# The down projection's left sums of a Winograd-Strassen scheme, formed in the gate and up stage instead of the down stage

## The chip, the cores and the metric

The kernel runs on one core of a Trainium2 chip. What counts is the device time of one execution, in microseconds (us): the median of the runs shown.

## What is computed

Two encoder layers on 1024 tokens of width 1024. Each has a token mixer (a Fourier part, a gated part, attention) and a channel mixer, of which this text speaks:

```python
def swiglu(h, w_gate, w_up, w_down):
    return (jax.nn.silu(h @ w_gate) * (h @ w_up)) @ w_down

x = x + rmsnorm(swiglu(rmsnorm(x, g_pre_ffn[l]), w_gate[l], w_up[l], w_down[l]), g_post_ffn[l])
```

The hidden width is 2816, that is 22 blocks of 128 or 11 pairs of blocks. All is float32.

## The kernel before

**Products.** A float32 operand is split into a high half (a rounding cast on ACT, L119) and a low half (operand minus high half, on DVE, L120). A product is three matmuls, high by high, high by low, low by high (`matmul3`, L142 to L144). `split` at L118 is used everywhere, so its two lines stand for all stages, and a tile's name tells which: `w_f` is a weight of gate or up, `dw` an operand of the down projection.

**Seven products for eight.** The three matrices of the channel mixer are multiplied by a Winograd form of Strassen's scheme: operands are cut into 2 x 2 blocks, sums and differences of blocks are formed, and seven products, numbered v = 1 to 7 in the down stage, replace eight.

**The gate and up stage.** `NPROD` = 154 products: 11 pairs `p`, each with j = 0 to 13 (v = j // 2, gate and up by turns). `ff_load` fetches the weights of a pair in four tiles from a pool of four buffers (`rawp`), `ff_sums` (L943) forms the sums of weight blocks on POOL, `ff_prep` splits a weight six products ahead into a pool of nine buffers (`Wp`), `ff_prod` multiplies into PSUM (`fx`, `fy`), `ff_post` empties the accumulators into slots of `nat` (L997, L1006), applies silu, multiplies gate by up and stores the four blocks of the pair's result in the DRAM tile `asp` (`store_a`, L974).

**The down stage.** The 11 pairs make four groups (3, 3, 3, 2 pairs). In each group the seven products go in the order v = 1, 2, 5, 6, 3, 7, 4: 28 steps (`STEPS`). A step is for each of four row blocks `u` one accumulator, with three matmuls for each pair of the group: 36 matmuls, 24 in the last group (`d_prod`). `X` accumulators (`fX`) are opened at v = 1, `Y` accumulators (`fY`) at v = 2 and anew at v = 5; there are four banks of each kind. They are emptied into `nat` on ACT (L1121) or added to it on DVE (L1123). `d_load` (L1051) fetches for each pair two tiles of 128 x 1024 of the left side, from `asp`, and two of `w_down`, into a ring of buffers of which four are those of `rawp`. `d_sums` (L1064) forms the sums on POOL, in place:

```python
                if v == 5:
                    tt(a(11), a(11), a(21))
                    tt(a(21), a(21), a(22), ALU.add)
                    tt(w(11), w(12), w(11))
                    tt(w(12), w(22), w(12))
                elif v == 6:
                    tt(a(21), a(22), a(11))
                    tt(w(11), w(22), w(11))
                elif v == 3:
                    tt(a(12), a(12), a(21))
                elif v == 4:
                    tt(w(21), w(21), w(11))
```

That is eight sums a pair, four of left blocks `a` and four of right blocks `w`. `d_prep(s + 3)` runs behind step s: it forms the sums of step s + 3 and splits its operands, two for each pair, into 18 buffers, so an operand's buffer is one that step s has just left.

**What sets the order.** The program's order as written, and a scheduler that orders each engine's instructions when the kernel is built; `run_behind` and `chain` pin some. Each engine, and SP's queue of DMA issues, then works through its list in order. In the last group, the final normalisation (`Residual`, L177 to L228) is woven into the steps by the table `FIN`.

Of the kernel before, what the change touches and what calls it, by code (L numbers as in the profile page):

```python
# [81 lines left out]
def encoder_kernel(ctx, tc, A, out):  # L82
# [273 lines left out]
    for l in range(DEPTH):  # L356
# [613 lines left out]
            pcn[0] += 1  # L970
            return nat[:, i, half * 512:(half + 1) * 512]

        def store_a(i, half, t):
            nc.sync.dma_start(asp[i * P:(i + 1) * P, half * 512:(half + 1) * 512], t)  # L974

        def ff_prod(n):
            p, j = divmod(n, 14)
# [11 lines left out]
        def ff_post(n):  # L989
            p, j = divmod(n, 14)  # L990
            v, m = j // 2, j % 2
            X = pq["X", p, m]

            def finish(key, acc, i, half):

                t = pq[key, p, m]
                nc.vector.tensor_tensor(out=t, in0=acc, in1=t, op=ALU.add)  # L997
                if m == 0:
                    nc.scalar.activation(t, t, AF.Silu)
                else:  # L1000
                    nc.vector.tensor_tensor(out=t, in0=pq[key, p, 0], in1=t, op=ALU.mult)
                    store_a(i, half, t)

            if v in (0, 3, 4):
                t = pq[("p1", None, None, "u2", "u3")[v], p, m] = pc()
                nc.scalar.copy(t, X)  # L1006
            if v == 1:
                finish("p1", pq["Y", p, m], 2 * p, 0)
            elif v == 4:
                finish("u3", pq["Z", p, m], 2 * p + 1, 1)  # L1010
            elif v == 5:
                if m == 0:
                    t = pq["s", p] = pc()
                    nc.scalar.activation(t, X, AF.Silu)
                else:
                    t = pq["s", p]
                    nc.vector.tensor_tensor(out=t, in0=X, in1=t, op=ALU.mult)
                    store_a(2 * p + 1, 0, t)
            elif v == 6:
                finish("u2", pq["Z", p, m], 2 * p, 1)  # L1020

        DGROUPS = ((0, 1, 2), (3, 4, 5), (6, 7, 8), (9, 10))
        DORD = (1, 2, 5, 6, 3, 7, 4)
        STEPS = [(gi, v) for gi in range(len(DGROUPS)) for v in DORD]
        draw, dop, dps, du = {}, {}, {}, {}
# [5 lines left out]
        RING = [("dR", i) for i in range(9)] + [("raw", 0)] * 4 + [("dM", i) for i in range(10)]  # L1033

        def d_raw_slot(gi, n):

            return RING[(12 * gi + n) % len(RING)]

        def d_load(gi, n):

            G = len(DGROUPS[gi])
            j, r = divmod(n, 2 * G)
            pi, side = divmod(r, 2)
            i = 2 * DGROUPS[gi][pi] + j
            kind, slot = d_raw_slot(gi, n)
            nm = f"dr{l}_{gi}_{n}"
            if kind == "raw":
                raw = rawp.tile([P, S], F32, tag="raw", name=nm)
            else:
                raw = d_unit(kind, slot, [S], F32, nm)  # L1050
            nc.sync.dma_start(raw, (A["w_down"][l] if side else asp)[i * P:(i + 1) * P, :])  # L1051
            draw[gi, pi, side, j] = raw

        def d_blk(gi, pi, side, b):

            r, c = divmod(b, 10)
            j, h = (c, r) if side == 0 else (r, c)
            return draw[gi, pi, side, j - 1][:, (h - 1) * 512:h * 512]

        def d_sums(gi, v):  # L1060
            for pi in range(len(DGROUPS[gi])):
                a = lambda b: d_blk(gi, pi, 0, b)
                w = lambda b: d_blk(gi, pi, 1, b)
                tt = lambda o, x, y, op=ALU.subtract: nc.gpsimd.tensor_tensor(out=o, in0=x, in1=y, op=op)  # L1064
# [12 lines left out]

        DOPER = {1: (11, 11), 2: (12, 21), 5: (21, 11), 6: (21, 11), 3: (12, 22), 7: (11, 12), 4: (22, 21)}

        def d_op_slot(s, n):  # L1080

            gi, v = STEPS[s]
            if len(DGROUPS[gi]) == 3:
                return ("W", "W", "W", "W", "W", "W", "W", "W", "W", ("dO", 0), ("dO", 1), ("dO", 2),
                        ("dO", 3), ("dN", 0), ("dN", 1), ("dN", 2), ("dN", 3), ("dN", 4))[s % 3 * 6 + n]
            return {1: "W", 2: "W", 5: ("dO", n), 6: ("dN", n), 3: ("dR", 4 + n), 7: ("dR", n), 4: ("dN", n)}[v]

        def d_prep(s):
            if s >= len(STEPS):
                return  # L1090
            gi, v = STEPS[s]
            d_sums(gi, v)
            n = 0
            for pi in range(len(DGROUPS[gi])):
                for side in range(2):
                    slot = d_op_slot(s, n)
                    nm = f"dw{l}_{s}_{n}"
                    if slot == "W":
# [82 lines left out]
        for n in range(NPROD):  # L1181
            p, j = divmod(n, 14)
            ff_prod(n)
            if n > 4:
                ff_post(n)
            if n in (0, 2):
                b_tp(6 + n // 2)
            for e in TSTEPS.get(n, ()):
                run_behind(e)
            if j in LOADS and p + 1 < NPAIR:  # L1190
                ff_load(p + 1, *LOADS[j])
            if n > 7:
                ff_prep(n + 6)
            if n == NPROD - 10:
                sB.close()
                sL = ExitStack()
                du["dR"] = pool(f"dR{l}", 1, "left", sL)
            if NPROD - 10 <= n < NPROD - 1:
                d_load(0, n - (NPROD - 10))
            if n == NPROD - 1:  # L1200
                for k in range(9, 12):
                    d_load(0, k)
        sT.close()


        last = l == DEPTH - 1
        sD = ExitStack()
        du["dO"] = pool(f"dO{l}", 1, "left", sL)
        du["dN"] = pool(f"dN{l}", 1, "right", sD)
        du["dM"] = pool(f"dM{l}", 1, "right", sD)  # L1210
        for s in range(3):
            d_prep(s)

        fin = {}

# [36 lines left out]
        for s, (gi, v) in enumerate(STEPS):  # L1252
            end = gi + 1 == len(DGROUPS)
            for u in range(4):
                if not (end and v == 4):
                    d_tile(s, u)
                if end and v == 7:
                    d_tile(s + 1, u)
            k = DORD.index(v)
            if not end and k < 4:  # L1260
                for n in range(k * 3, min(k * 3 + 3, 4 * len(DGROUPS[gi + 1]))):
# [49 lines left out]
```

## Time and profile before

| | |
|---|---|
| median of 3 runs | 2284.11 us (2282.67 to 2284.31) |
| the profiled execution | 2282.25 us, span 2280.5 us |
| PE busy | 2191.5 us, 96% of the span |
| DVE busy | 1607.3 us, 70% |
| ACT busy | 1138.5 us, 50% |
| POOL busy | 952.2 us, 42% |
| DMA queue of SP | 178.70 MB, 23.1% of 16 engines' span |

Engines: PE is TensorE's matmuls, DVE is VectorE, ACT is ScalarE, POOL is GpSimd, SP is SyncE, which issues the DMAs. Matmuls are pipelined, so one of 0.39 us starts every 0.23 us and a busy PE is not PE at its peak: how many matmuls start in a stretch tells more. The first layer's gate and up stage runs from about 460 to 894 us, its down stage to about 1115; the second layer's down stage begins at about 2028. The rows are at the end of this part.

### The profile page before, as it was taken

Reading aid. Unit: us, or ns where it says so; the run is one execution under the profiler, and the core shown is the slowest. Engines: PE = TensorE matmul, PEld = TensorE weight load, DVE = VectorE, ACT = ScalarE, POOL = GpSimd, SP = SyncE. Lnnn points to the kernel's source line nnn. Section 1 sums busy time; section 2 is a strip of 40 time slices with the busy share of each in tenths; the row PEclk is TensorE's granted clock in tenths of the full one; section 3 lists DMA queues with packets and bytes.
Section 4 is the critical chain, followed back from the end, with each engine's and each line's share of the span. In section 5 each row is a group of like instructions: output and inputs, shape, how many; then the busy total and the mean of one; then the engine's idle time right before and its main releaser. Section 6 shows DMA issues by size and latency. Waiting matters only on the chain. (4 is left out here: it accounts for less than half of the span.)

```text
span 2280.5 us, 29159 instructions
## 1 busy us (share of the span) xinstructions
PE 2191.5 (96%) x10460; PEld 1807.2 (79%) x10460; DVE 1607.3 (70%) x2457; ACT 1138.5 (50%) x2188; POOL 952.2 (42%) x797
## 2 busy tenths in 40 slices
PE   9999999999999999999899999999999999999986
PEld 7787888878888888877677788888788888877874
DVE  6868986585444447899977698965854444488998
ACT  6338996553333334434452489855533333344333
POOL 2643443243323235655637235332432323266556
PEclk9999999999999999999999999999999999999998
DMA  4110003213132316221331000042132323253212
GB/s 159 42 45 20 19 10 115 99 65 106 61 105 62 104 62 240 111 84 47 107 111 38 17 19 20 10 138 85 61 102 74 93 74 93 74 226 111 83 47 111
DMA packets 104961, 185.28 MB, mean 81 GB/s; under 512 B 12272, under 2 KB 62704, under 8 KB 104816
## 3 DMA queue, kind: packets, MB, share of 16 engines
q1 hardware_dynamic: 103376, 178.70, 23.1%
q0 software_dynamic: 1440, 4.72, 0.7%
q8 instruction: 82, 1.34, 0.2%
q14 instruction: 63, 0.52, 0.1%
HBM read 143.54 MB, written 39.85 MB: 80 GB/s over the span
## 5 line engine op out<-in xcount | busy, mean ns | idle before, releaser
L144 PE MATMUL fx<-hT,w_f 128*128 128x512 f32 x1584 | 374.9, 393 | 6.6 <-ACT nat L1006 4.5
L144 PEld LDWEIGHTS fx<-hT,w_f 128*128 128x128 f32 x1584 | 300.1, 190 | 71.2 <-ACT nat L1006 6.0
L120 DVE TENSOR_TENSOR w_f<-raw_f,w_f 128x512 fp32r<-128x512 f32 x264 | 213.9, 814 | 192.6 <-ACT w_f L119 189.5
L120 DVE TENSOR_TENSOR dw<-dr,dw 128x512 fp32r<-128x512 f32 x300 | 325.4, 1129 | 30.2 <-ACT dw L119 29.9
L144 PE MATMUL z<-w_z,hT 128*128 128x512 f32 x1152 | 286.3, 403 | 11.8 <-DVE rz L196 5.1
L119 ACT CAST dw<-dr 128x512 fp32r<-128x512 f32 x308 | 171.8, 618 | 234.5 <-POOL dr L1064 94.1
L119 ACT CAST w_f<-raw_f 128x512 fp32r<-128x512 f32 x264 | 162.2, 621 | 236.3 <-PE fy L144 196.7
L144 PEld LDWEIGHTS z<-w_z,hT 128*128 128x128 f32 x1152 | 216.6, 193 | 58.6 <-DVE rz L196 5.5
L144 PE MATMUL fX<-dw,dw 128*128 128x512 f32 x1056 | 248.5, 391 | 8.8 <-DVE nat L1123 8.5
L943 POOL TENSOR_TENSOR s<-raw_f,raw_f 128x512 f32<-128x512 f32 x44 | 58.9, 1338 | 459.5 <-DMA raw_f<-in_w_gate_dram 442.1
L144 PE MATMUL fy<-hB,w_f 128*128 128x512 f32 x1056 | 248.0, 390 | 1.9 <-DVE hB L120 1.9
L144 PEld LDWEIGHTS fX<-dw,dw 128*128 128x128 f32 x1056 | 197.1, 188 | 54.8 <-DVE nat L1123 13.9
L144 PEld LDWEIGHTS fy<-hB,w_f 128*128 128x128 f32 x1056 | 198.0, 188 | 43.6 <-DVE hB L120 2.7
L1064 POOL TENSOR_TENSOR dr<-dr,dr 128x512 f32<-128x512 f32 x132 | 220.0, 1696 | 8.6 <-DVE dw L120 8.6
L144 PE MATMUL fY<-dw,dw 128*128 128x512 f32 x792 | 198.3, 408 | 24.1 <-DVE nat L1123 19.3
L997 DVE TENSOR_TENSOR nat<-fy,nat 128x512 f32<-128x512 f32 x132 | 90.9, 690 | 172.3 <-PE fy L144 88.2
L144 PEld LDWEIGHTS fY<-dw,dw 128*128 128x128 f32 x792 | 156.3, 199 | 61.8 <-DVE nat L1123 21.0
L120 DVE TENSOR_TENSOR pT<-ptr,pT 128x512 fp32r<-128x512 f32 x256 | 171.8, 685 | 35.9 <-ACT pT L119 33.5
L752 PE MATMUL pv<-pT,vv 128*128 128x512 f32 x512 | 181.0, 434 | 0.3 <-DVE pT L120 0.3
L119 ACT CAST pT<-ptr 128x512 fp32r<-128x512 f32 x256 | 150.6, 595 | 40.4 <-PE ptr L740 38.1
L1006 ACT COPY nat<-fx 128x512 f32<-128x512 f32 x132 | 77.6, 588 | 183.4 <-PE fx L144 177.7
L723 DVE TENSOR_REDUCE mx<-sc 128x1 f32<-128x1024 f32 x128 | 155.9, 1220 | 10.9 <-PE sc L720 8.9
(208 smaller groups left out, 3746.5 us busy)
## 6 DMA issues: line engine op xcount, KB each, us to landing
raw_f<-in_w_gate_dram SPq DMA_DIRECT2D x44, 512.0 KB, 3.6
raw_f<-in_w_up_dram SPq DMA_DIRECT2D x44, 512.0 KB, 4.1
asp<-nat SPq DMA_DIRECT2D x88, 256.0 KB, 2.6
dr<-in_w_down_dram SPq DMA_DIRECT2D x44, 512.0 KB, 6.1
dr<-asp SPq DMA_DIRECT2D x44, 512.0 KB, 6.5
xin<-xs SPq DMA_DIRECT2D x24, 512.0 KB, 3.3
raw_z<-in_w_in_dram SPq DMA_DIRECT2D x16, 512.0 KB, 4.1
raw_wo<-in_w_out_dram SPq DMA_DIRECT2D x16, 512.0 KB, 3.7
```

The lines of the kernel that those rows point to most:

```text
L119: nc.scalar.copy(hi, src)
L120: eng.tensor_tensor(out=lo, in0=src, in1=hi.bitcast(F32), op=ALU.subtract)
L144: nc.tensor.matmul(ps, lhs(a), rhs(b), start=first and i == 0, stop=last and i == 2, **kw)
L723: nc.vector.tensor_reduce(mx, sc, axis=AX.X, op=ALU.min)
L752: nc.tensor.matmul(pv, vv[:, kt, g].rearrange("p i d -> p (i d)"), pT[:, i], start=(kt == 0 and i == 0), stop=(kt == 7 and i == 1))
L943: tt = lambda o, x, y, op: nc.gpsimd.tensor_tensor(out=o, in0=x, in1=y, op=op)
L997: nc.vector.tensor_tensor(out=t, in0=acc, in1=t, op=ALU.add)
L1006: nc.scalar.copy(t, X)
L1064: tt = lambda o, x, y, op=ALU.subtract: nc.gpsimd.tensor_tensor(out=o, in0=x, in1=y, op=op)
```

## The change

The four left sums of a pair leave `d_sums` and become `left_sums(p)`, on POOL too. It is called at j = 6 of the next pair of the gate and up stage; the last pair's call stands behind the preparation of the first three down steps. The sums are formed in place in the slots of `nat` that hold the pair's gate products, and each is stored at once. `asp` now holds seven left operands of 128 x 512 for a pair instead of four blocks, ordered by group, product and pair, so that all left operands of a step lie together. The block a22 is stored as it is used only itself, a21 only in sums.

In the down stage `d_left(s)` loads one tile of up to 3 x 512 columns for a step, six steps ahead by the program, into four buffers. `d_load` fetches `w_down` alone, six tiles a group by turns into two pools `wE` and `wO`. The buffers of `rawp` are no longer used by the down stage. Splits, products and adds stay as they are.

```diff
-    asp = dram.tile([DFF, S], F32, name="asp")
+    asp = dram.tile([NFF // 2 * 7 * P, 512], F32, name="asp")
...
+        def left_sums(p):
+            a11, a12, a21, a22 = pq["p1", p, 1], pq["s", p], pq["u2", p, 1], pq["u3", p, 1]
+            s1, s2, s3 = pq["u2", p, 0], pq["u3", p, 0], pq["p1", p, 0]
+            tt = lambda o, x, y, op: nc.gpsimd.tensor_tensor(out=o, in0=x, in1=y, op=op)
+            tt(s1, a21, a22, ALU.add)
+            store_a(p, 5, s1)
+            tt(s2, s1, a11, ALU.subtract)
+            store_a(p, 6, s2)
+            tt(s3, a11, a21, ALU.subtract)
+            store_a(p, 7, s3)
+            tt(a21, a12, s2, ALU.subtract)
+            store_a(p, 3, a21)
...
-            nc.sync.dma_start(raw, (A["w_down"][l] if side else asp)[i * P:(i + 1) * P, :])
+            raw = d_unit("wE" if gi % 2 == 0 else "wO", n, [S], F32, f"dr{l}_{gi}_{n}")
+            nc.sync.dma_start(raw, A["w_down"][l, i * P:(i + 1) * P, :])
...
+        def d_left(s):
+            if s < len(STEPS):
+                gi, v = STEPS[s]
+                G = len(DGROUPS[gi])
+                t = du["wE"].tile([P, 3, 512], F32, tag="left", name=f"da{l}_{s}", bufs=4)
+                nc.sync.dma_start(t[:, 0:G], asp[asp_rows(gi, v, 0, G), :].rearrange("(g p) n -> p g n", p=P))
+                dleft[s] = t
...
                 if v == 5:
-                    tt(a(11), a(11), a(21))
-                    tt(a(21), a(21), a(22), ALU.add)
                     tt(w(11), w(12), w(11))
                     tt(w(12), w(22), w(12))
                 elif v == 6:
-                    tt(a(21), a(22), a(11))
                     tt(w(11), w(22), w(11))
-                elif v == 3:
-                    tt(a(12), a(12), a(21))
                 elif v == 4:
                     tt(w(21), w(21), w(11))
...
+            if j == 6 and p:
+                left_sums(p - 1)
...
+            if n >= NPROD - 10:
+                k = n - (NPROD - 10)
+                run((d_load, 0, k) if k < 6 else (d_left, k - 6))
...
         for s in range(3):
             d_prep(s)
+        left_sums(NPAIR - 1)
+        d_left(4)
+        d_left(5)
...
             d_prep(s + 3)
+            d_left(s + 6)
```

How the instruction lists move is seen at three places. In the names, `dr_g_n` is raw tile n of group g, `da_s` the left tile of step s, `dw_s_n` operand n of step s (even n left, odd n right), `fY_s_u` an accumulator opened at step s, `raw_f_p_m_h` a gate or up weight tile, `raw_z` an input weight tile of the next layer. Steps count from 0 here.

SP's queue at the end of the first layer's gate and up stage, before:

```order
L974 DMA asp<-nat 128x512 x2
L1051 DMA dr_0_9_7964<-in_w_down_dram 128x1024
L1051 DMA dr_0_10_7966<-asp 128x1024
L974 DMA asp<-nat 128x512
L1051 DMA dr_0_0_7810<-asp 128x1024
L1051 DMA dr_0_1_7829<-in_w_down_dram 128x1024
```

and in the changed kernel:

```order
L301 DMA raw_z_0_0_9511<-in_w_in_dram 128x2x256 x2
L301 DMA raw_z_0_1_9514<-in_w_in_dram 128x2x256 x2
L984 DMA asp<-nat 128x512 x4
L301 DMA raw_z_0_2_9517<-in_w_in_dram 128x2x256
L984 DMA asp<-nat 128x512
L301 DMA raw_z_0_2_9517<-in_w_in_dram 128x2x256
L301 DMA raw_z_0_3_9520<-in_w_in_dram 128x2x256 x2
L1062 DMA dr_0_0_7872<-in_w_down_dram 128x1024
```

The freed buffers of `rawp` now take the next layer's input weights, and their loads stand ahead of the first `w_down` tile; the last `raw_z` tile needs the buffer of the last gate/up weight tile. Six `w_down` tiles and then the left tiles follow. In the second layer four residual tiles stand in the place of `raw_z`.

DVE's list ahead of the add that frees the first accumulator for the third step, before (the low halves shown begin at the third step's second operand):

```order
L120 TENSOR_TENSOR dw_2_1_8031<-dr_0_1_7829,dw_2_1_8031 128x512
L120 TENSOR_TENSOR dw_2_2_8034<-dr_0_2_7847,dw_2_2_8034 128x512
L120 TENSOR_TENSOR dw_2_3_8037<-dr_0_3_7865,dw_2_3_8037 128x512
L120 TENSOR_TENSOR dw_2_4_8040<-dr_0_4_7882,dw_2_4_8040 128x512
L120 TENSOR_TENSOR dw_2_5_8043<-dr_0_5_7900,dw_2_5_8043 128x512
L120 TENSOR_TENSOR dw_3_0_8102<-dr_0_0_7810,dw_3_0_8102 128x512
L120 TENSOR_TENSOR dw_3_1_8105<-dr_0_1_7829,dw_3_1_8105 128x512
L120 TENSOR_TENSOR dw_3_2_8108<-dr_0_2_7847,dw_3_2_8108 128x512
L120 TENSOR_TENSOR dw_3_3_8111<-dr_0_3_7865,dw_3_3_8111 128x512
L1123 TENSOR_TENSOR nat<-fY_1_0_8120,nat 128x512
```

and in the changed kernel, from the last post-processing of the gate and up stage on:

```order
L1025 TENSOR_TENSOR nat<-nat 128x512
L128 TENSOR_TENSOR dw_1_3_8069<-dr_0_4_7952,dw_1_3_8069 128x512
L128 TENSOR_TENSOR dw_1_4_8072<-da_1_8001,dw_1_4_8072 128x512
L128 TENSOR_TENSOR dw_1_5_8075<-dr_0_5_7970,dw_1_5_8075 128x512
L128 TENSOR_TENSOR dw_2_0_8084<-da_2_8017,dw_2_0_8084 128x512
...
L128 TENSOR_TENSOR dw_2_5_8099<-dr_0_2_7917,dw_2_5_8099 128x512
L128 TENSOR_TENSOR dw_3_0_8165<-da_3_8033,dw_3_0_8165 128x512
L128 TENSOR_TENSOR dw_3_1_8168<-dr_0_0_7872,dw_3_1_8168 128x512
L128 TENSOR_TENSOR dw_3_2_8171<-da_3_8033,dw_3_2_8171 128x512
L1136 TENSOR_TENSOR nat<-fY_1_0_8185,nat 128x512
```

Between the gate and up stage's last multiplication on DVE and the add now stand twelve low halves, where nine stood.

POOL's list at the same boundary in the changed kernel:

```order
L990 TENSOR_TENSOR nat<-nat 128x512 x4
L1082 TENSOR_TENSOR dr_0_0_7872<-dr_0_0_7872 128x512
L1082 TENSOR_TENSOR dr_0_1_7891<-dr_0_1_7891 128x512
L1082 TENSOR_TENSOR dr_0_0_7872<-dr_0_3_7935,dr_0_0_7872 128x512
L1082 TENSOR_TENSOR dr_0_2_7917<-dr_0_2_7917 128x512
L1082 TENSOR_TENSOR dr_0_1_7891<-dr_0_4_7952,dr_0_1_7891 128x512
L1082 TENSOR_TENSOR dr_0_2_7917<-dr_0_5_7970,dr_0_2_7917 128x512
L990 TENSOR_TENSOR nat<-nat 128x512 x3
L1082 TENSOR_TENSOR dr_0_0_7872<-dr_0_3_7935,dr_0_0_7872 128x512
L990 TENSOR_TENSOR nat<-nat 128x512
```

The last pair's left sums (the second L990) stand behind the third step's six right sums; before, twelve sums of both sides stood there.

## Rows read from the trace of the kernel before

**Rows 1.** The page's head and section 1

```profile
span 2280.5 us, 29159 instructions
PE 2191.5 (96%) x10460; PEld 1807.2 (79%) x10460; DVE 1607.3 (70%) x2457; ACT 1138.5 (50%) x2188; POOL 952.2 (42%) x797
```

**Rows 2.** Stretches of 10 us: their length, then each engine's busy us (instructions), clock, DMA share, GB/s

```profile
570.00:580.00 10.00, 10.00 (x46) 8.29 (x45) 3.72 (x5) 3.49 (x7) 8.27 (x6) 1.00 0.02 6
...
2060.00:2070.00 10.00, 10.00 (x46) 8.29 (x45) 5.08 (x8) 4.88 (x9) 0.00 (x0) 1.00 1.00 360
...
2100.00:2110.00 10.00, 5.73 (x24) 4.45 (x23) 10.00 (x11) 4.04 (x7) 10.00 (x7) 0.87 0.00 0
...
2170.00:2180.00 10.00, 5.40 (x15) 4.27 (x16) 10.00 (x13) 3.93 (x7) 6.76 (x5) 0.66 0.01 2
```

**Rows 3.** Timeline of PE, second layer's down stage: start us, us, what, times [idle before]

```profile
2028.47 6.96 PE L144 MATMUL fX<-dw,dw 128*128 128x512 f32 x30
2035.28 8.32 PE L144 MATMUL fY<-dw,dw 128*128 128x512 f32 x36
2045.97 10.00 PE L144 MATMUL fY<-dw,dw 128*128 128x512 f32 x36 [2.37 <-ACT dw L119]
2055.81 8.32 PE L144 MATMUL fX<-dw,dw 128*128 128x512 f32 x36
2063.97 8.32 PE L144 MATMUL fY<-dw,dw 128*128 128x512 f32 x36
...
2109.42 10.71 PE L144 MATMUL fY<-dw,dw 128*128 128x512 f32 x36 [4.27 <-DVE nat L1123]
2119.97 8.10 PE L144 MATMUL fX<-dw,dw 128*128 128x512 f32 x35
...
2174.60 10.54 PE L144 MATMUL fY<-dw,dw 128*128 128x512 f32 x36 [4.86 <-DVE nat L1123]
2184.98 7.87 PE L144 MATMUL fX<-dw,dw 128*128 128x512 f32 x34
...
2261.28 1.67 PE L144 MATMUL fX<-dw,dw 128*128 128x512 f32 x6 [0.50 <-DVE nat L1123]
```

**Rows 4.** Groups by line: busy us, mean ns | idle before and who ended it

```profile
L120 DVE TENSOR_TENSOR dw<-dr,dw 128x512 fp32r<-128x512 f32 x300 | 325.4, 1129 | 30.2 <-ACT dw L119 29.9
...
L1064 POOL TENSOR_TENSOR dr<-dr,dr 128x512 f32<-128x512 f32 x132 | 220.0, 1696 | 8.6 <-DVE dw L120 8.6
```

**Rows 5.** Timelines of DVE and POOL, first layer's down stage

```profile
899.21 13.15 DVE L120 TENSOR_TENSOR dw<-dr,dw 128x512 fp32r<-128x512 f32 x9
912.28 0.68 DVE L1123 TENSOR_TENSOR nat<-fY,nat 128x512 f32<-128x512 f32 x1
...
918.55 2.48 DVE L120 TENSOR_TENSOR dw<-dr,dw 128x512 fp32r<-128x512 f32 x4
...
950.77 14.78 DVE L120 TENSOR_TENSOR dw<-dr,dw 128x512 fp32r<-128x512 f32 x9
...
953.06 26.81 POOL L1064 TENSOR_TENSOR dr<-dr,dr 128x512 f32<-128x512 f32 x16
```

**Rows 6.** Timeline of POOL, one pair of the first layer's gate and up stage

```profile
568.17 1.29 POOL L943 TENSOR_TENSOR s<-raw_f,raw_f 128x512 f32<-128x512 f32 x1 [24.42 <-DMA raw_f<-in_w_gate_dram]
...
580.54 1.29 POOL L943 TENSOR_TENSOR raw_f<-raw_f,raw_f 128x512 f32<-128x512 f32 x1 [1.99 <-DVE w_f L120]
606.33 1.29 POOL L943 TENSOR_TENSOR s<-raw_f,raw_f 128x512 f32<-128x512 f32 x1 [24.51 <-DMA raw_f<-in_w_gate_dram]
```

**Rows 7.** First layer's stage boundary: timelines of PE, SP and DVE, one stretch

```profile
895.62 6.96 PE L144 MATMUL fX<-dw,dw 128*128 128x512 f32 x30
...
863.30 0.38 SPq L1051 DMA_DIRECT2D dr<-asp  x1
...
870.71 0.69 DVE L120 TENSOR_TENSOR w_f<-raw_f,w_f 128x512 fp32r<-128x512 f32 x1 [1.43 <-ACT w_f L119]
...
874.00:876.00 2.00, 2.00 (x11) 1.65 (x10) 2.00 (x3) 0.99 (x3) 1.67 (x1) 1.00 1.03 414
```

More of the change, by code (lines that the diff above doesn't have):

```diff
@@ L114, in encoder_kernel, with asp_rows @@
     xs = dram.tile([S, D], F32, name="xs")
[L115 removed]
+    asp = dram.tile([NFF // 2 * 7 * P, 512], F32, name="asp")
+    DGROUPS = ((0, 1, 2), (3, 4, 5), (6, 7, 8), (9, 10))
+    DORD = (1, 2, 5, 6, 3, 7, 4)
+    def asp_rows(gi, v, pi, n=1):
+        b = 7 * DGROUPS[gi][0] + DORD.index(v) * len(DGROUPS[gi]) + pi
+        return slice(b * P, (b + n) * P)
     def split(hi, lo, src, eng=nc.vector):
@@ L971, in pc, with store_a @@
             return nat[:, i, half * 512:(half + 1) * 512]
-        def store_a(i, half, t):
-            nc.sync.dma_start(asp[i * P:(i + 1) * P, half * 512:(half + 1) * 512], t)
+        def store_a(p, v, t):
+            gi = min(p // 3, len(DGROUPS) - 1)
+            nc.sync.dma_start(asp[asp_rows(gi, v, p - DGROUPS[gi][0]), :], t)
+        def left_sums(p):
[10 more added lines that the diff above has]
+            store_a(p, 3, a21)
         def ff_prod(n):
@@ L992, in ff_post, with finish @@
             X = pq["X", p, m]
-            def finish(key, acc, i, half):
+            def finish(key, acc, dv=None):
                 t = pq[key, p, m]
@@ L1001, in finish @@
                     nc.vector.tensor_tensor(out=t, in0=pq[key, p, 0], in1=t, op=ALU.mult)
-                    store_a(i, half, t)
+                    if dv:
+                        store_a(p, dv, t)
             if v in (0, 3, 4):
@@ L1031, in d_unit, with d_blk @@
             return p.tile([P] + shape, dt, tag=f"{kind}{i}", name=name, bufs=1)
-        RING = [("dR", i) for i in range(9)] + [("raw", 0)] * 4 + [("dM", i) for i in range(10)]
-        def d_raw_slot(gi, n):
-            return RING[(12 * gi + n) % len(RING)]
         def d_load(gi, n):
             G = len(DGROUPS[gi])
-            j, r = divmod(n, 2 * G)
-            pi, side = divmod(r, 2)
+            j, pi = divmod(n, G)
             i = 2 * DGROUPS[gi][pi] + j
[L1045 to L1050, printed above, removed]
-            nc.sync.dma_start(raw, (A["w_down"][l] if side else asp)[i * P:(i + 1) * P, :])
-            draw[gi, pi, side, j] = raw
-        def d_blk(gi, pi, side, b):
+            raw = d_unit("wE" if gi % 2 == 0 else "wO", n, [S], F32, f"dr{l}_{gi}_{n}")
+            nc.sync.dma_start(raw, A["w_down"][l, i * P:(i + 1) * P, :])
+            draw[gi, pi, j] = raw
+        def d_left(s):
[5 more added lines that the diff above has]
+                dleft[s] = t
+        def d_blk(gi, pi, b):
             r, c = divmod(b, 10)
-            j, h = (c, r) if side == 0 else (r, c)
-            return draw[gi, pi, side, j - 1][:, (h - 1) * 512:h * 512]
+            return draw[gi, pi, r - 1][:, (c - 1) * 512:c * 512]
         def d_sums(gi, v):
             for pi in range(len(DGROUPS[gi])):
-                a = lambda b: d_blk(gi, pi, 0, b)
-                w = lambda b: d_blk(gi, pi, 1, b)
-                tt = lambda o, x, y, op=ALU.subtract: nc.gpsimd.tensor_tensor(out=o, in0=x, in1=y, op=op)
+                w = lambda b: d_blk(gi, pi, b)
+                tt = lambda o, x, y: nc.gpsimd.tensor_tensor(out=o, in0=x, in1=y, op=ALU.subtract)
                 if v == 5:
-                    tt(a(11), a(11), a(21))
-                    tt(a(21), a(21), a(22), ALU.add)
                     tt(w(11), w(12), w(11))
@@ L1101, in d_prep @@
                         t = d_unit(slot[0], slot[1], [2, 512], R32, nm)
-                    split(t[:, 0], t[:, 1], d_blk(gi, pi, side, DOPER[v][side]), nc.gpsimd if gi + 1 == len(DGROUPS) and v in (3, 4) and pi else nc.vector)
+                    split(t[:, 0], t[:, 1], d_blk(gi, pi, DRIGHT[v]) if side else dleft[s][:, pi], nc.gpsimd if gi + 1 == len(DGROUPS) and v in (3, 4) and pi else nc.vector)
                     dop[s, pi, side] = t
@@ L1196, in encoder_kernel @@
                 sL = ExitStack()
[L1197 to L1202, printed above, removed]
+                du["wE"] = pool(f"dE{l}", 1, "left", sL)
+            if n >= NPROD - 10:
+                k = n - (NPROD - 10)
+                run((d_load, 0, k) if k < 6 else (d_left, k - 6))
         sT.close()
@@ L1207, in encoder_kernel @@
         sD = ExitStack()
-        du["dO"] = pool(f"dO{l}", 1, "left", sL)
-        du["dN"] = pool(f"dN{l}", 1, "right", sD)
-        du["dM"] = pool(f"dM{l}", 1, "right", sD)
+        du["wO"] = pool(f"dO{l}", 1, "right", sD)
+        du["op"] = pool(f"dP{l}", 1, "right", sD)
         for s in range(3):
             d_prep(s)
+        left_sums(NPAIR - 1)
+        d_left(4)
+        d_left(5)
         fin = {}
@@ L1260, in encoder_kernel @@
             if not end and k < 4:
-                for n in range(k * 3, min(k * 3 + 3, 4 * len(DGROUPS[gi + 1]))):
+                for n in range(k * 2, min(k * 2 + 2, 2 * len(DGROUPS[gi + 1]))):
                     d_load(gi + 1, n)
             d_prep(s + 3)
+            d_left(s + 6)
             if end and v == 1:
```

20 lines of the change are left out of this document (9 added, 11 removed).

## The prediction

> **What bounds the kernel now.** I read the page first: the span is 2280.5 us and TensorE is busy for 96% of it [rows 1]. What another engine saves counts only where it makes TensorE wait, so the next view is the stretches of 10 us [rows 2]. In the gate and up stage (570 to 580) and early in the down stage (2060 to 2070) 46 matmuls start per 10 us at a granted clock of 1.00. In 2100 to 2110 only 24 do and in 2170 to 2180 only 15; in both VectorE is busy for all 10 us, GpSimd for 10 and 6.8, and the clock stands at 0.87 and 0.66. The down stage's stops are thus to be measured on TensorE's own timeline of the second layer [rows 3].
>
> A step of a group of three pairs is 36 matmuls; from 2055.81 to 2063.97 one takes 8.16 us, 0.2267 us a matmul. The stage has 924, of which 918 stand after 2028.47: 208.1 us without a stop. They end at 2261.28 + 1.67 = 2262.95, after 234.5 us, so 26.4 us are lost, in four places [rows 3]. **Start:** the third step could begin at 2035.28 + 8.16 = 2043.44 and begins at 2045.97, then takes 9.84 instead of 8.16 us, since the clock has dropped: 4.2 us. **Second group:** 4.4 us of waiting before 2109.42 and 10.55 instead of 8.16 us after it: 6.8. **Third group:** 5.0 before 2174.60, 2.2 after it and 0.3 of a small gap: 7.5. **Last group and end:** the 310 matmuls from 2184.98 need 70.3 us and take 78.0: 7.7. The bracket at 2109.42 and 2174.60 names VectorE's L1123, the add that empties the accumulator. The first layer shows the same four.
>
> Why is that add late? A low half (the subtraction of L120 that splits an operand) takes 1129 ns in the mean [rows 4]. Four in a row with GpSimd idle take 2.48 us, 0.60 each; nine in a row take 14.78 us, 1.64 each, while GpSimd's sums run, at 26.81 / 16 = 1.68 us instead of the 1.29 of one alone [rows 5, 6]. The nine lost 14.78 - 5.4 = 9.4 us to 8.8 sums, so **a GpSimd sum costs VectorE about 1.05 us** if low halves stand ready. The add of L1123 takes 0.68 us even in the midst of GpSimd's sums [rows 5]: only the low halves suffer. All stops but the start follow from that load. A new group's third product needs accumulators that the second's adds free. Between TensorE's start of the step before last of a group and the next group's third step lie five steps, 40.8 us; VectorE owes 24 low halves and 17 adds in them, 41 x 0.61 = 25.0 us, and the 24 sums of a group add 24 x 1.05 = 25.2. 50.2 us of work in 40.8 predicts some 9 us of lateness, an upper end since not every sum meets low halves; 4.4 and 5.0 us are seen, and the slow clock behind them.
>
> The Trainium skill, "SBUF — State Buffer", section "Who interferes with whom", says that a VectorE instruction with two SBUF inputs and a GpSimd instruction that reads SBUF exclude each other for the whole instruction, while one SBUF input does not contend. The rows agree on the add (one input is PSUM), and differ in size: 1.05 us lost per sum against the 1.29 of a full lock. By the rule a group after the change would need 25.0 + 12 x 1.29 = 40.5 us of the 40.8; by the row it needs less (below). The row decides.
>
> **The change, part by part.** Removed from the down stage: per layer 44 of GpSimd's 88 sums. Added in the gate and up stage: the same 44, four for each pair.
>
> *Second and third group.* VectorE now owes 25.0 + 12 x 1.05 = 37.6 us in 40.8. The stop has no cause left: -6.8 and -7.5 us. Bounds: all of it, or half, if the remaining sums still bunch just ahead of the add (its place in VectorE's order behind low halves is unchanged).
>
> *Last group.* Its steps have 24 matmuls; 8 of 16 sums go, 8.4 us of VectorE's time, against 5.9 us lost up to 2250. The rest, 1.8 us at the very end, is between final norms and adds, which the change does not touch. I leave 3.0 of the 7.7: -4.7. Bounds: 1.8 and 7.7 left.
>
> *Start.* Here the change adds a wait. SyncE issues in order. Before, the first right factors and left rows go out from 863.30 [rows 7]. Now the next layer's input weights (in the second layer the residual rows) take the four buffers that the left and right rows used, stand ahead of the right factors in SyncE's order, and the last needs a buffer that is free only after the low half of the last gate/up weight, 870.71 + 0.69 = 871.4 [rows 7]. The first right factor leaves some 9 us later, at about 872.3. Ahead of the first left tile lie half a MB of weights, 3.1 MB of right factors and 0.8 MB of its own; at 414 GB/s [rows 7] it lands at about 883. The gate/up products end at 895.62 - 6 x 0.2267 = 894.3, as the six early down matmuls now come behind them. The casts of step one start at 884, its low halves end at about 892: in time. But casts of step two then wait for weight buffers of the last three products, until 894.3; VectorE reaches the fourth low half of step two at about 899, and 12 of them stand ahead of the add that frees the first accumulator for step three. GpSimd runs beside them most of the time: six sums of step three, then the last pair's four left sums, which wait for the last product, then those of step four. At 1.64 us for some nine and 0.6 for three this is 16.6 us, and the add ends at about 916.7. Step three could start at 894.3 + 16.3 = 910.6 and 0.3 for a late step two. Before, nine low halves started at 899.21 and the add ended at 912.96 [rows 5]. So 5.8 us of wait and 1.7 of slow clock: 7.5 where 4.2 were, **+3.3 us**. Bounds: 2 (if few sums meet low halves), and 4.2 + 9 = 13.2, the whole delay of the loads.
>
> *Later loads.* A left tile is asked for four steps ahead of its split, over 20 us, against landing times of a few us: nothing. Without that cover a step would wait for 0.8 MB, 2 us.
>
> *Left sums and stores, gate and up stage.* GpSimd's eight sums of a pair end at 580.54 + 1.29 = 581.8, and its next work is at 606.33, when a load has landed [rows 6]. Four sums at 1.29 to 1.68 end by 588.6. VectorE loses 4.2 us per pair where it is half idle [rows 2]; weights are split six products ahead, so TensorE sees nothing; 46 matmuls in 10 us stand in the very stretch with 8.27 us of GpSimd work [rows 2]. The four stores wait for GpSimd ahead of the next weight load on SyncE, but that load waits for a buffer until shortly before 606: 14 us or more of cover. 33 more stores of 256 KB per layer use a queue that is mostly idle. Cost: 0; without the cover, what GpSimd is late by, per pair.
>
> **Sum.** Per layer -6.8 - 7.5 - 4.7 + 3.3 = -15.7 us; the first layer loses as much in the same places, so -31.4. The profiled run took 2282.25 us (1.75 around the span), 1.9 below the median of 2284.11; a difference carries over: **2253 us**.
>
> **The rivals.** *A, the sum above,* 0.50.
>
> *B, the start loses little* (2 us a layer): low halves are then done before GpSimd's left sums begin. For it: GpSimd idles while it waits for the last product. Per layer -21.2: 2242 us. 0.15.
>
> *C, the start takes the whole delay of the loads,* 13.2 us: smaller packets of the stored sums land later than I reckon, or the last pair's sums hold the casts. Per layer -10.0: 2264 us; with nothing won in the last group 2273. 0.12.
>
> *D, the order keeps half of the stops:* the add still stands behind nine to twelve low halves, and the group's 12 sums run just then. 3.4 and 3.7 us stay: -8.6 a layer, 2267 us. Against it: three us of slack in 40.8. 0.12.
>
> *E, slower: the gate and up stage pays.* Place: SyncE's queue, where four stores wait for GpSimd ahead of a weight load. If GpSimd finished its left sums after the load's buffer is free, each pair would start late. The gain of 15.7 us a layer is used up at 1.4 us for each of 11 pairs, for which the sums would have to run 14 + 1.4 us later than reckoned; at 2.5 us a pair the kernel takes 2308 us. The idle stretch to 606.33 speaks against it. 0.06.
>
> *F, no difference:* the load moved is not what holds the add, or start and stops cancel: 2284 us. 0.05.
>
> **How the numbers follow.** About 0.2% (4.6 us) is what a measurement of this kernel can tell from no change. A to D are all faster: 0.89, less 0.02 for a C that ends near zero: faster 0.87, same 0.06, slower 0.07. The range takes in B's 2242 with the last group at its bound (-1.2 a layer more: 2239.6) and C's 2273: 2238 to 2274. Left out are E, F and extremes, under 2 in 10.
>
> **What would show it.** Right: low halves of the down stage near 0.95 us in the mean; the waits for L1123 in the second and third group gone, the clock at 1.00 there; 46 matmuls per 10 us from the down stage's fourth step on; a stop of 4 to 7 us at its third step, larger than before; GpSimd's work per pair of gate and up at 12 sums with TensorE never waiting. Wrong: TensorE waiting in the gate and up stage; the first left tile landing after 895; a wait for the same add in later groups of over 2 us; or GpSimd's remaining sums holding casts.

## The result, and the profile after

The changed kernel takes 2253.22 us (median of 4 runs, 2251.03 to 2254.12) against 2283.7 before (4 runs, 2282.67 to 2284.31; the table ahead has three of them): ratio 0.9864, 95% interval 0.9853 to 0.9876. The profiled execution took 2253.72 us, 28.5 less than the one before. (In the kernel before, the first layer's down stage ends at 1129.82 us, not at about 1115 as the text ahead says.)

The head of the page and its first section, changed kernel:

```profile
span 2252.0 us, 29256 instructions
...
PE 2179.4 (97%) x10460; PEld 1802.8 (80%) x10460; DVE 1567.7 (70%) x2457; ACT 1135.5 (50%) x2188; POOL 932.3 (41%) x797
```

The matmuls are the same in number, and TensorE is busy for 12 us less, since slow matmuls count as busy too. The stops are read from its timeline in the second layer's down stage (start us, us, what, times, idle before it and what ended that), which answers to [rows 3]:

```profile
2012.79 8.32 PE L152 MATMUL fX<-dw,dw 128*128 128x512 f32 x36
2020.95 8.32 PE L152 MATMUL fY<-dw,dw 128*128 128x512 f32 x36
2035.83 7.17 PE L152 MATMUL fY<-dw,dw 128*128 128x512 f32 x18 [6.56 <-DVE nat L1136]
2042.84 0.39 PE L152 MATMUL fX<-dw,dw 128*128 128x512 f32 x1
2043.07 4.26 PE L152 MATMUL fY<-dw,dw 128*128 128x512 f32 x18
2047.17 8.10 PE L152 MATMUL fX<-dw,dw 128*128 128x512 f32 x35
...
2096.13 8.32 PE L152 MATMUL fY<-dw,dw 128*128 128x512 f32 x36
...
2153.47 8.32 PE L152 MATMUL fY<-dw,dw 128*128 128x512 f32 x36
...
2185.89 9.68 PE L152 MATMUL fX<-dw,dw 128*128 128x512 f32 x42
...
2231.12 3.33 PE L152 MATMUL fX<-dw,dw 128*128 128x512 f32 x12 [1.78 <-DVE nat L1136]
```

The stage's first matmul starts at 2012.79. Steps one and two need 16.32 us, so step three could begin at 2029.11; it begins at 2035.83, after 6.56 us of waiting for the add of L1136 (L1123 before). Its 36 matmuls and the one at 2042.84 need 8.39 us and take 11.34 to 2047.17: the clock again (0.58 in the stretch from 2030 to 2040 below). So **the start loses 9.7 us**, where it lost 4.2. From 2047.17 to 2185.89 stand 612 matmuls, 138.7 us at 0.2267, and they take 138.72: **groups two and three lose nothing**, where they lost 14.3. The rows at 2096.13 and 2153.47 are the v = 5 steps that waited before, now without a bracket. The end, 2231.12 + 3.33 = 2234.45, lies 221.66 us after the start; 924 matmuls need 209.5; so 12.2 us are lost, and **2.5 are left for the last group**, where it was 7.7.

Stretches of 10 us (length, busy us of each engine with instructions, clock, DMA share, GB/s), for [rows 2]:

```profile
570.00:580.00 10.00, 10.00 (x45) 8.27 (x45) 2.68 (x3) 2.84 (x5) 7.25 (x6) 1.00 0.36 123
2030.00:2040.00 10.00, 4.17 (x10) 3.33 (x11) 10.00 (x12) 4.90 (x10) 6.21 (x4) 0.58 0.37 120
2090.00:2100.00 10.00, 10.00 (x46) 8.27 (x45) 9.57 (x16) 3.23 (x6) 0.81 (x1) 1.00 0.23 80
2150.00:2160.00 10.00, 10.00 (x46) 8.29 (x45) 8.71 (x16) 3.23 (x6) 0.00 (x0) 1.00 0.35 107
```

The third and fourth rows lie where groups two and three stood still: 46 matmuls at a clock of 1.00. The start has 10, at 0.58. The first row lies in the gate and up stage. (Such a count, here and in [rows 2], takes in the matmuls still under way when the stretch begins; at 0.2267 us each, 44.1 start in 10 us.) The groups by line (busy us, mean ns, idle before), for [rows 4]:

```profile
L128 DVE TENSOR_TENSOR dw<-dr,dw 128x512 fp32r<-128x512 f32 x150 | 147.7, 985 | 0.0
...
L128 DVE TENSOR_TENSOR dw<-da,dw 128x512 fp32r<-128x512 f32 x150 | 130.8, 872 | 32.4 <-ACT dw L127 32.0
...
L1082 POOL TENSOR_TENSOR dr<-dr,dr 128x512 f32<-128x512 f32 x66 | 107.6, 1644 | 41.1 <-DVE dw L128 39.8
```

Low halves now take (985 + 872) / 2 = 928 ns in the mean, where they took 1129. Those of left operands are quicker than those of right operands; why isn't shown.

### The profile page after: what moved, and what is told of

Same layout as the page of the kernel before. It is cut to its first block, busy times and chain, and to the rows that moved or that the text cites. A ratio compares the mean times of both kernels' runs of the same rounds, so it can differ in the third digit from the quotient of the medians.

```text
span 2252.0 us, 29256 instructions
## 1 busy us (share of the span) xinstructions
PE 2179.4 (97%) x10460; PEld 1802.8 (80%) x10460; DVE 1567.7 (70%) x2457; ACT 1135.5 (50%) x2188; POOL 932.3 (41%) x797
## 5 line engine op out<-in xcount | busy, mean ns | idle before, releaser
L128 DVE TENSOR_TENSOR w_f<-raw_f,w_f 128x512 fp32r<-128x512 f32 x264 | 229.6, 874 | 182.7 <-ACT w_f L127 179.8
L990 POOL TENSOR_TENSOR nat<-nat 128x512 f32<-128x512 f32 x88 | 134.7, 1552 | 277.9 <-ACT w_f L127 262.5
L152 PE MATMUL fY<-dw,dw 128*128 128x512 f32 x792 | 191.6, 398 | 13.9 <-DVE nat L1136 13.9
L127 ACT CAST dw<-da 128x512 fp32r<-128x512 f32 x154 | 94.9, 619 | 153.7 <-PE fY L152 71.4
L748 PE MATMUL ptr<-identr,pj 128*128 128x128 f32 x1024 | 154.5, 273 | 0.9 <-ACT pj L741 0.9
L128 DVE TENSOR_TENSOR dw<-da,dw 128x512 fp32r<-128x512 f32 x150 | 130.8, 872 | 32.4 <-ACT dw L127 32.0
```

Of the source, the lines that this page charges most:

```text
L152: nc.tensor.matmul(ps, lhs(a), rhs(b), start=first and i == 0, stop=last and i == 2, **kw)
L748: nc.tensor.transpose(tr[:, j * P:(j + 1) * P], ast["p", G, j][:, kt * P:(kt + 1) * P], ident)
L990: tt = lambda o, x, y, op: nc.gpsimd.tensor_tensor(out=o, in0=x, in1=y, op=op)
```

## The experiments

Each starts from the changed kernel unless it says otherwise. A single run of these kernels carries some 2 to 3 us of chance: in the changed kernel's profile the first layer's attention, which no edit touches, ends 1.8 us later than before, and the second layer's takes 2.0 us less. In the twelve traces an attention takes between 190.5 and 192.7 us. So stops are compared by their own rows, the totals only where they differ by more.

**Spare sums.** Does a GpSimd sum that nobody waits for bring the stops back?

```diff
+        def spare(x):
+            nc.gpsimd.tensor_tensor(out=scr[:, 0], in0=x, in1=scr[:, 1], op=ALU.subtract)
...
         def d_prep(s):
...
+            for pi in range(len(DGROUPS[gi])):
+                for _ in range({5: 2, 6: 1, 3: 1}.get(v, 0)):
+                    spare(dleft[s][:, pi])
             d_sums(gi, v)
```

> The changed kernel, with four extra sums per pair put back on GpSimd in the down stage, at v = 5 (two), 6 and 3. They read the step's left tile and a scratch tile and write a scratch tile that nobody reads. Theory 1 (a GpSimd sum slows VectorE's low halves by about 1 us, and the add that empties the accumulator comes late for that): low halves of the down stage back from 0.93 to about 1.1 us in the mean, the waits of 4 to 5 us ahead of the v = 5 step of the second and third group back, the last group and the start worse too: 2253 + 2 x (14.3 + 5.2) = about 2292 us, 2278 to 2305. Rival 1 (the change won because operands no longer wait for a left sum, or because of the new loads; the slowing is beside the point): nothing waits for these sums, so 2253 to 2258 us and no stops in groups two and three.

2292.4 us, in one run beside 2284.62 for the kernel before. Its groups by line:

```profile
L128 DVE TENSOR_TENSOR dw<-dr,dw 128x512 fp32r<-128x512 f32 x150 | 180.8, 1207 | 11.6 <-ACT dw L127 11.3
...
L128 DVE TENSOR_TENSOR dw<-da,dw 128x512 fp32r<-128x512 f32 x150 | 167.6, 1118 | 8.6 <-ACT dw L127 8.6
...
L1102 POOL TENSOR_TENSOR scr<-da,scr 128x512 f32<-128x512 f32 x88 | 141.8, 1611 | 109.5 <-DMA da<-asp 105.8
```

and on TensorE's timeline the v = 5 step of the second group in both layers, and of the third in the second layer:

```profile
985.30 4.92 PE L152 MATMUL fY<-dw,dw 128*128 128x512 f32 x14 [6.24 <-DVE nat L1142]
...
2122.06 8.29 PE L152 MATMUL fY<-dw,dw 128*128 128x512 f32 x29 [6.24 <-DVE nat L1142]
...
2185.80 9.37 PE L152 MATMUL fY<-dw,dw 128*128 128x512 f32 x33 [2.42 <-DVE nat L1142]
```

(The counts in TensorE's rows end at the edge of the stretch shown.) Low halves take 1163 ns in the mean, and TensorE waits for the add where it waited before the change: 6.24 us in the second group, where 4.27 stood, and 2.71 and 2.42 in the third, where 4.85 and 4.86 stood. Counted as above, the two groups lose 15.2 us in the first layer and 16.4 in the second, as against 14.3 before the change. Nothing reads what these sums write. Theory 1 holds; rival 1 falls.

**Spare fills.** Is it GpSimd's time, or what a sum does to VectorE? Against the run with spare sums:

```diff
-            nc.gpsimd.tensor_tensor(out=scr[:, 0], in0=x, in1=scr[:, 1], op=ALU.subtract)
+            nc.gpsimd.tensor_tensor(out=scr[:, 0, 0:8], in0=x[:, 0:8], in1=scr[:, 1, 0:8], op=ALU.subtract)
+            nc.gpsimd.memset(scr, 0.0)
+            nc.gpsimd.memset(scr[:, 0], 0.0)
```

> As the run with spare sums, but each spare sum is replaced by a fill of 128x1024 and one of 128x512 elements on GpSimd (with a tiny sum of 8 columns ahead that ties it to the step): by the 0.2 us that a fill of 128x128 takes, some 1.5 us, as long as a sum, in the same places of GpSimd's order, but hardly reading SBUF. Theory 1: VectorE's low halves stay near 0.93 us, no stops in groups two and three, 2253 to 2260 us. Rival 2 (what counts is GpSimd's own time: right sums come late behind a longer list, so casts and low halves wait for them): the same stops and the same time as with spare sums, about 2292 us. If fills slow VectorE as sums do, the two runs agree as well, and the low halves' mean tells which of the two it is.

2254.23 us. Groups by line:

```profile
L128 DVE TENSOR_TENSOR dw<-dr,dw 128x512 fp32r<-128x512 f32 x150 | 140.0, 936 | 1.4 <-ACT dw L127 1.4
L128 DVE TENSOR_TENSOR dw<-da,dw 128x512 fp32r<-128x512 f32 x150 | 136.8, 913 | 31.4 <-ACT dw L127 31.0
...
L1103 POOL MEMSET scr<- 128x1024 f32 x88 | 84.1, 956 | 4.4
...
L1104 POOL MEMSET scr<- 128x512 f32 x88 | 46.4, 527 | 3.9
...
L1102 POOL TENSOR_TENSOR scr<-da,scr 128x8 f32<-128x8 f32 x88 | 38.2, 435 | 48.1 <-DMA da<-asp 42.8
```

The fills and their small sums hold GpSimd for 84.1 + 46.4 + 38.2 = 168.7 us, more than the spare sums' 141.8, in the same steps; the low halves stay at 925 ns and the stops of groups two and three away. Rival 2 falls: it is not GpSimd's time but the reading sum beside the low half. 47 low halves ran beside a fill and no sum: they took 683 ns in the mean, as did 48 that ran beside neither. Between the two runs low halves differ by 348.4 - 276.8 = 71.6 us, 0.81 us for each of the 88 sums. The Trainium skill, "SBUF — State Buffer", section "Who interferes with whom", restricts the exclusion to GpSimd instructions that read SBUF; fills and sums here agree with that (683 ns beside a fill, up to 1.78 us beside a sum).

**No left sums at all**, from the kernel before: the floor.

```diff
-                    tt(a(11), a(11), a(21))
-                    tt(a(21), a(21), a(22), ALU.add)
...
-                    tt(a(21), a(22), a(11))
...
-                elif v == 3:
-                    tt(a(12), a(12), a(21))
```

> The kernel before, with its four left sums per pair left out of the down stage (so its output leaves the left sums out: blocks are used as loaded); loads, buffers and all else as before. Theory 1: the stops of groups two and three go and most of the last group's, and the start is a little better than before, with loads that go out early and six sums less: 2283.7 - 2 x (14.3 + 5.2) = 2244.7, less 0 to 6: 2238 to 2246 us. It is then the floor for the change, and the changed kernel's 2253 stands above it by what its start costs. Rival 1 (the new loads and buffers win): the stops stay and the time is above 2270 us.

2235.29 us, 2.7 below the range expected. Groups two and three lose nothing, the last group 1.0 and 1.7 us; and at the start the third step (TensorE's timeline, both layers) waits next to nothing:

```profile
911.93 8.44 PE L144 MATMUL fY<-dw,dw 128*128 128x512 f32 x36 [0.42 <-ACT dw L119]
...
2021.00 8.43 PE L144 MATMUL fY<-dw,dw 128*128 128x512 f32 x36 [0.43 <-ACT dw L119]
```

With the small loss in the step itself the start loses 0.7 us a layer. So the kernel before lost 3.5 of its 4.2 us there to the left sums as well. The changed kernel stands 18 us above this floor, and its two starts, 9.7 - 0.7 = 9.0 us each, make up as much.

**Triple left sums.** Is the gate and up stage really free?

```diff
+            R = 3 if p < NPAIR - 1 else 1
...
-            tt(s1, a21, a22, ALU.add)
+            for _ in range(R):
+                tt(s1, a21, a22, ALU.add)
```

(likewise for the other three)

> The changed kernel, with each left sum of the first ten pairs of a layer formed three times over in the gate and up stage (same result), so 12 instead of 4 sums there, 12.2 us more of GpSimd's time per pair and 8 x 1.05 = 8.4 us more for VectorE. Theory 1 (the stage has cover: GpSimd idles for 14.6 + 5.1 us around its left sums, VectorE is half idle): 46 matmuls per 10 us throughout, 2251 to 2256 us. Rival 3 (the stage pays for what GpSimd does there, by the stores ahead of the weight loads or by late low halves of weights): from 1.4 us a pair, 28 us, to 8 us a pair, 2280 to 2410 us, with TensorE waiting in the gate and up stage.

2255.86 us. From 520 to 860 us, 28 of 34 stretches of 10 us hold 46 matmuls and 6 hold 45, the same counts as in the changed kernel. The cover stands at three times the load; rival 3 falls. What is added stands at the stage's end, where low halves come late for the first down steps (waits of up to 2.40 us): the start loses 11.2 and 10.2 us instead of 9.7. The changed kernel's own GpSimd timeline shows the room, for [rows 6]:

```profile
561.01 6.10 POOL L990 TENSOR_TENSOR nat<-nat 128x512 f32<-128x512 f32 x4 [14.62 <-ACT w_f L127]
572.22 1.29 POOL L951 TENSOR_TENSOR s<-raw_f,raw_f 128x512 f32<-128x512 f32 x1 [5.11 <-DMA raw_f<-in_w_gate_dram]
...
583.17 1.28 POOL L951 TENSOR_TENSOR raw_f<-raw_f,raw_f 128x512 f32<-128x512 f32 x1 [1.02 <-DVE w_f L128]
599.09 6.11 POOL L990 TENSOR_TENSOR nat<-nat 128x512 f32<-128x512 f32 x4 [14.63 <-ACT w_f L127]
```

**The start.** What holds its add? Four edits look for it. In the changed kernel, SyncE's first right tile, ACT's first cast, VectorE's last low halves and GpSimd beside them, first layer:

```profile
875.19 3.51 SPq L1062 DMA_DIRECT2D dr<-in_w_down_dram  x6
878.75 5.95 SPq L1071 DMA_DIRECT2D da<-asp  x4
...
889.00 0.62 ACT L127 CAST dw<-da 128x512 fp32r<-128x512 f32 x1 [2.20 <-DMA da<-asp]
...
914.40 1.75 DVE L128 TENSOR_TENSOR dw<-da,dw 128x512 fp32r<-128x512 f32 x1
916.07 1.74 DVE L128 TENSOR_TENSOR dw<-dr,dw 128x512 fp32r<-128x512 f32 x1
917.74 1.75 DVE L128 TENSOR_TENSOR dw<-da,dw 128x512 fp32r<-128x512 f32 x1
919.42 0.68 DVE L1136 TENSOR_TENSOR nat<-fY,nat 128x512 f32<-128x512 f32 x1
...
912.20 8.43 POOL L1082 TENSOR_TENSOR dr<-dr,dr 128x512 f32<-128x512 f32 x5
```

The first left tile is awaited until 889.00. From its first low half, at 889.65, VectorE is never idle until the add at 919.42, and the low halves that meet a GpSimd sum take 1.74 to 1.78 us, but for one of 1.19.

*Loads first:*

```diff
-            nc.sync.dma_start(raw[:, :, o:o + n], rows2(A["w_in"][l], kk * 256, c0, n))
+            with ExitStack() as e:
+                if c == 0 and l:
+                    e.enter_context(tc.issue_after(mark[0]))
+                nc.sync.dma_start(raw[:, :, o:o + n], rows2(A["w_in"][l], kk * 256, c0, n))
...
-            fin[t] = Residual(t, t // 4, fin["gpost"], xs, out if last else xs, xin, None, f"po{l}_{t}")
+            with tc.issue_after(mark[0]):
+                fin[t] = Residual(t, t // 4, fin["gpost"], xs, out if last else xs, xin, None, f"po{l}_{t}")
```

(`mark[0]` is the DMA of the fourth left tile)

> The changed kernel, with the next layer's input weights (second layer: the residual rows) held on SyncE's queue behind the first six right tiles and four left tiles of the down stage, so that these go out some 9 us earlier, near 863 as before. The start loses 9.7 us a layer in the changed kernel. Theory 4 (the late loads cost it: casts of the first step wait for the first left tile until 889, and VectorE's whole chain to the add is late by that): the chain starts 6 to 9 us earlier, the loss falls to 0 to 3 us, 2234 to 2240 us. Rival 4 (GpSimd's sums beside VectorE, the last pair's left sums among them, and operand buffers that come free only with the last products at 894, set the add's time, wherever the loads are): the loss stays at 7 to 10 us, 2248 to 2254 us.

2246.3 us. SyncE's first right tile and TensorE's third step, first layer:

```profile
871.30 3.01 SPq L1065 DMA_DIRECT2D dr<-in_w_down_dram  x6
...
916.70 6.02 PE L152 MATMUL fY<-dw,dw 128*128 128x512 f32 x18 [5.37 <-DVE nat L1139]
```

The wait falls from 6.78 to 5.37 us; of the 7.4 us between the two profiled runs 2.1 stand ahead of the first layer's down stage, 1.3 of them ahead of its gate and up stage, where no edit reaches. The first right tile went out at 871.30, not near 863: stores that wait for GpSimd's left sums stood ahead of it. Measured to TensorE's first down matmul (896.89 and 894.84), the first cast came 2.3 us earlier (889.00 and 884.64), and the start lost 2.4 us less. Neither theory as put; so the stores were moved too.

*Loads ahead of the stores:*

```diff
+            d = lambda: nc.sync.dma_start(asp[asp_rows(gi, v, p - DGROUPS[gi][0]), :], t)
+            if late is not None and (p == NPAIR - 1 or p == NPAIR - 2 and v in (5, 6, 7, 3)):
+                late.append(d)
+            else:
+                d()
```

(`late` is issued behind the fourth left tile)

> As the run with the loads first, where the first right tile still went out at 871.3 only (875.2 in the changed kernel), since stores of the last two pairs, which wait for GpSimd, stood ahead of it on SyncE; here these stores stand behind the first left tiles too, so that the loads go out near 863. Theory 4 (the late loads cost the start its whole 9.7 us): the loss falls to 0 to 1 us, 2234 to 2236 us. Mixed theory (an earlier chain helps only until the operand buffers run out, which come free with the last products; GpSimd's sums do the rest): nine low halves are done before 888, the others wait for buffers, the add comes some 3 us after TensorE could use it, loss 4 to 5 us, 2242 to 2244 us. No more than the loads-first run, 2246: the load was not the limit any more.

2249.12 us, with the same stop (the start loses 7.2 and 7.3 us):

```profile
862.13 6.25 SPq L1070 DMA_DIRECT2D dr<-in_w_down_dram  x6
...
883.90 0.59 ACT L1039 COPY nat<-fx 128x512 f32<-128x512 f32 x1 [0.74 <-PE fx L152]
884.38 0.62 ACT L127 CAST dw<-da 128x512 fp32r<-128x512 f32 x1
...
916.45 5.90 PE L152 MATMUL fY<-dw,dw 128*128 128x512 f32 x18 [5.39 <-DVE nat L1144]
```

The loads now go out at 862.13, 9 us before the run above, and nothing is won, against theory 4 and against the 4 to 5 us of the mixed theory: ACT's list has the first cast behind a copy that waits for TensorE's product until 883.90. So **of the 9.7 us the late loads cost 2.4**, and then a list order takes over.

*Last pair raw:*

```diff
-            tt = lambda o, x, y, op: nc.gpsimd.tensor_tensor(out=o, in0=x, in1=y, op=op)
+            tt = lambda o, x, y, op: nc.gpsimd.tensor_tensor(out=o, in0=x, in1=y, op=op) if p < NPAIR - 1 else None
```

> The changed kernel, without the last pair's four left sums of each layer, which GpSimd forms in the midst of the start (this leaves them out of the result: the last pair's products use the slots as they are); their stores stay. By the 1.05 us that a sum costs VectorE, the add comes up to 4.2 us earlier: the start loses 5 to 6 us instead of 9.7, 2244 to 2247 us. If these sums lie beside other waits (casts, buffers), no difference: 2252 to 2254 us.

2246.31 us. TensorE's second and third step, first layer:

```profile
903.38 8.32 PE L152 MATMUL fY<-dw,dw 128*128 128x512 f32 x36
916.10 10.66 PE L152 MATMUL fY<-dw,dw 128*128 128x512 f32 x36 [4.39 <-DVE nat L1136]
```

The third could start at 903.38 + 8.16 = 911.54 and starts at 916.10; then it takes 10.49 to the next step instead of 8.16. So 6.9 us are lost, where 5 to 6 were expected: 2.8 fewer than 9.7, for four sums, 0.7 us each. The total lies in the range expected with the help of chance, since two starts account for 5.6 of the 7 us.

*Adds first:*

```diff
-            d_prep(s + 3)
+            if s > 1:
+                d_prep(s + 3)
+            elif s == 1:
+                with ExitStack() as e:
+                    for eng in (nc.vector, nc.gpsimd, nc.scalar):
+                        e.enter_context(tc.issue_after(...))
+                    d_prep(3)
...
+                    d_prep(4)
```

(`issue_after` takes the engine's last instruction so far; the second block is like the first)

> The changed kernel, with the four adds that empty the first accumulators placed ahead of the low halves of the fourth step in VectorE's order (only at the start of each down stage); loads as they are. The add then stands behind three low halves less, which took 1.67 to 1.7 us each beside GpSimd's sums. If the start's stop is the add's place behind slow low halves, the add comes 5 us earlier, the stop shrinks from 7.0 to about 2 us, the clock drop with it, and the fourth step's operands are ready about in time: 9.7 falls to 2 to 4 us a layer, 2238 to 2243 us. If what follows is late instead (the fourth step waits for its own low halves), the loss stays near 9 us: 2250 to 2255 us.

2237.73 us, 0.3 under the range expected. TensorE's timeline, the third step of both layers:

```profile
913.27 4.38 PE L152 MATMUL fY<-dw,dw 128*128 128x512 f32 x18 [1.72 <-DVE nat L1136]
...
2022.65 4.38 PE L152 MATMUL fY<-dw,dw 128*128 128x512 f32 x18 [1.56 <-DVE nat L1136]
```

1.72 and 1.56 us of waiting where 6.78 and 6.56 stood, and no clock drop behind them: 18 matmuls take 4.38 us, not 7.17. The down stages are 7.5 and 7.8 us shorter. The fourth step doesn't wait. The edit pins GpSimd's sums and ACT's casts for the fourth step too, but that isn't what won: in both kernels the nine low halves ahead of the first add take 12.0 us (902.40 to 914.40 in the changed kernel, 900.54 to 912.54 here). The three low halves that stood behind them took 5.0 us (914.40 to 919.42 above); the rest of the 7.5 is the clock drop that didn't come.

**Loads first and adds first:**

> The changed kernel with both edits: the down stage's first loads ahead of the next layer's weights, and the first adds ahead of the fourth step's low halves. If each of the two takes away its own part of the lateness, the start loses 0 to 2 us a layer, 2234 to 2239 us, near the 2235 us of the kernel without left sums in the down stage. If they remove the same lateness, the time is that of the better of the two.

2236.3 us (4 runs, 2233.52 to 2237.43), 0.9785 of the kernel before (0.9768 to 0.9801); the wait is 0.26 us in both layers, and the start loses 0.6. **Loads first, loads ahead of the stores and adds first:**

> The three edits together (loads ahead of the weights, loads ahead of the stores, adds ahead of the fourth step's low halves). The kernel with the first and the third has 0.4 us left at the start; so if the start is all there is to win, 2234 to 2237 us, the same as that one.

2232.92 us (4 runs, 2232.51 to 2234.13), 0.9778 of the kernel before (0.9761 to 0.9794): the best version, 20 us below the changed kernel. It too waits 0.26 us, here in the first layer:

```profile
911.46 4.37 PE L152 MATMUL fY<-dw,dw 128*128 128x512 f32 x18 [0.26 <-DVE nat L1144]
```

The 3.4 us between these two don't lie at the starts, and their intervals overlap. Of the 4.9 us between their profiled runs 3.7 stand in the token mixers, 1.9 of these in the two attentions, and 1.1 in the second gate and up stage. That looks like chance; it isn't shown.

## Why the prediction was right, by its own steps

**Second and third group: right in size and cause.** -14.3 us a layer foretold; they lose nothing now, so -14.3 measured. The spare sums and fills show the cause: GpSimd's sums that read SBUF slow the low halves ahead of the add. Rival D had nothing: neither v = 5 step waits. The price of 1.05 us is what a sum costs where low halves stand ready (1.75 - 0.68 = 1.07 in the rows of the start); averaged over all sums it was 0.81 (spare sums) and 0.7 (last pair).

**Last group: right.** -4.7 foretold, -5.2 measured; 2.5 us are left.

**Gate and up stage at no cost: right.** Without the six early down matmuls of before, that stage grew by 0.8 us in the first layer and shrank by 0.2 in the second; even three times the sums stayed hidden. Rival E falls. But the cover is not the one that was named. The prediction let the left sums begin right behind the weight sums and end 14 us or more ahead of the next load. They begin 14.6 us later than that and end 5 us before GpSimd's next work (584.45 to 599.09, and 567.11 to 572.22, in the rows above). A load of gate weights now stands behind the stores that wait for them, on SyncE's queue; before and in the changed kernel:

```profile
564.07 0.37 SPq L129 DMA_DIRECT2D raw_f<-in_w_gate_dram  x1
...
567.69 0.38 SPq L137 DMA_DIRECT2D raw_f<-in_w_gate_dram  x1
```

It leaves 3.62 us later than before. The pair's other loads and TensorE's matmuls are 2.64 later from there on, a shift that stands before the sums matter; so this load is 1.0 us late in each later pair of the first layer. Rival E's delay came true at its place, and TensorE doesn't wait for it. The cost of nought was right; the 14 us of cover on SyncE's queue were not, and there luck had a part.

**Start: right in kind, too small in size.** +3.3 foretold, +5.5 measured (4.2 to 9.7): the one term that was mis-sized. The first right tile left at 875.19, not 872.3, and the first left tile was used at 889.0, not 883. The add ended 23.2 us after the stage's start, not 22.4 (899 + 16.6 and 0.7 for the add itself make 916.3, so the 916.7 has 0.4 more than the terms given). TensorE began step three 6.7 to 7.0 us late, not 5.8, and the slow clock took 2.6 to 2.9, not 1.7. The prediction named the late loads as what starts the chain; they cost 2.4 us. The larger lever is the add's place behind three low halves of the fourth step, worth 7.5 with the clock. It saw that place and priced it, but took it as given. Rival B, a start that loses 2 us, falls with the 9.7 measured. Rival C, where the whole delay of the loads is lost, falls with the run that sent them out at 862. Rival F, no difference, falls with the result.

**The sum.** -15.7 us a layer foretold, -14.2 and -14.5 measured; the profiled run should have gained 31.4 and gained 28.5. That 2253 and 2253.22 lie so close is partly chance: the medians, 30.5 apart, differ by more than the two profiled runs.

## What to carry to other kernels

Count what a helper engine costs the engine beside it, not only its own time: here 44 sums a layer of 1.3 to 1.7 us each were named by no wait of TensorE, yet moving them to a stage with slack gave 14 us a layer. A moved load's place in a queue matters only up to the next list order that holds its reader. When a wait names an instruction, see what stands ahead of it in its engine's order: putting four adds ahead of six low halves was worth as much as half of the whole change.

## What the runs showed of the hardware that was not expected

A low half of the down stage mostly takes one of three times: about 0.68 us, or beside a GpSimd sum about 1.2 or 1.75 (211, 27 and 48 of the 300 in the changed kernel). In the rows of the start above, five sums of GpSimd take 8.43 us, 1.69 each, and low halves start every 1.67 us: the two take turns. A turn is 0.2 us shorter than 0.60 + 1.29 = 1.89, the two alone one after the other, so by this estimate the exclusion covers nearly all of an instruction. The 0.68 us add that reads PSUM stays at 0.68 in the midst of it, and fills on GpSimd cost a low half nothing that shows (683 ns with and without).
